# hl 32 bytes later, and the two weight slots apart by 64 bytes modulo 128

## The chip, the cores and the metric

The kernel runs on one core of one Trainium2 chip. The metric is the device time of one execution in microseconds, the median of several runs. The core has five engines with a queue each: TensorE (PE, with PEld for the loading of weights into the array), VectorE (DVE), ScalarE (ACT), GpSimd (POOL) and SyncE (SP, which here only issues DMAs). The working memory (SBUF) has 128 partitions; a tile takes the same bytes of each, and this case is about the byte at which a tile begins in its partition.

## The reference

One encoder layer (D_MODEL 1024, depth 1) is applied to two sequences of 1024 tokens, each with a conditioning vector. Cut to what matters:

```
mod = silu(c) @ w_ada + b_ada ; shift, scale, gate = split(mod, 3)
h = rmsnorm(x, norm_g) * (1 + scale) + shift
a_b, a_c, a_x, a_z, q, k, v, b_z, lr_f, lr_b, m_a, m_b = split(h @ w_in)
y_a = (a_b * conv3(a_c * a_x) * silu(a_z)) @ w_a_out
o = gla(q, k, v, g_f) + flip(gla(flip(q), flip(k), flip(v), flip(g_b), strict))
y_b = (rmsnorm(o) * gla_norm_g * silu(b_z)) @ w_b_out
x = x + gate * ((sigmoid(m_a) * y_a + sigmoid(m_b) * y_b) @ w_out)
y = rmsnorm(x, final_norm_g)
```

`gla` is a gated linear attention with 4 heads (keys of 128, values of 256 per head), g_f and g_b its log decays from a low-rank product. All is float32.

## The kernel before

Every large product is made in three matmuls on float32r operands: a float32 value is split into a high part (rounded by ScalarE, L114) and a low part (the rest, subtracted by VectorE or GpSimd, L115). `product` (L127) issues for each 128 rows of the contraction `hi.hi` (L131), `hi.lo` (L132) and `lo.hi` (L133); the first operand is the weights that are loaded into the array, the second the moving one. `mm3` (L135) runs it over the 8 blocks k of the model dimension.

- **hh and hl** (L97, L98) are the high and low parts of the modulated h, features in the partitions, 8 x 1024 float32 each, 32 KB a partition. They live through the whole kernel: for sequence 0, then 1, and at the end they hold w_out. `h_act` gives the slices.
- **w** (L118, `load_w`): 128 output columns of a weight matrix at a time, loaded into `raw` (three slots, by SP's queue), split into w's high and low half, 4 KB each. The tag "w" has two slots (NW), used in turn. `halves` (L141) makes one such tile's product with 2 x 512 tokens: for each 512 tokens 24 matmuls of 128 weight columns by 512 moving columns into one PSUM bank, so 48 matmuls use one slot. `wlr` (L427) is a narrow tile of the same tag.
- **big and small** (L66, L69): ten slots of 8 KB and eight of 4 KB, for all else: wv (values' weights, which are the moving operand there, with hh and hl as weights and 256 columns), b (the operands of the output products in `merge`, L691), mg (weights in `final`, L740), V, kt, As, SB, SF, Q (attention), wf and wa (start).
- **ones** and ident are constants, in a pool of their own ahead of hh. `over_features` (L166) sums over the partitions by a matmul with ones as weights.

The order of the work: `start` (modulation, h of sequence 0, and the first products as h arrives), then for each sequence `mixers` (four heads; each head's projections, then its attention, into which steps of the convolution's projections, `dense`, are woven) and `merge` (output products and gates, while h of the next user is filled into hh and hl), then `final`. A tile framework allocates the pools one tag after the other in the order in which they first appear, and makes every wait from what the tiles read and write. Weights are prefetched by giving `load_w` a higher priority.

Of the kernel before, what the change touches and what calls it, by code (L numbers as in the profile page):

```python
# [11 lines left out]
F32 = mybir.dt.float32  # L12
F32R = mybir.dt.float32r
# [4 lines left out]
P = 128  # L18
D = 1024
KT = D // P  # L20
L = 1024
# [16 lines left out]
NBIG, NSMALL, NW, NRAW = 10, 8, 2, 3  # L38
# [13 lines left out]
def encoder_kernel(ctx, tc, x_p, x_s, x_t, weights, w_lr, w_gate, w_out, vectors, b_gate, final_norm_g, masks, y_p, y_s):  # L52
# [6 lines left out]
    sb = ctx.enter_context(tc.tile_pool(name="sb", bufs=1))  # L59
# [35 lines left out]
    mk = const.tile([P, len(MASKED), P], U8, name="mk")  # L95
    sel = sb.tile([4, 2], F32, name="sel")
    hh = sb.tile([P, KT, L], F32R, name="hh")  # L97
    hl = sb.tile([P, KT, L], F32R, name="hl")  # L98

    ta_d = [dram.tile([KT, P, L], F32, name=f"ta_d{s}") for s in range(2)]  # L100
# [5 lines left out]
    def staged(src, shape=(P, L), queue=lambda load: None):  # L106

        raw = sb.tile(list(shape), F32, name="raw", tag="raw", bufs=NRAW)
        queue(nc.sync.dma_start(out=raw, in_=src))
        return raw  # L110

    def split(hi, lo, raw, engine):

        high = nc.scalar.copy(out=hi, in_=raw)  # L114
        engine.tensor_sub(out=lo, in0=raw, in1=hi.bitcast(F32))  # L115
        return high

    def load_w(i, shape=(KT, P), w=None, **kw):  # L118

        with tc.high_priority(offset=30):  # L120
            if w is None:
                w = sb.tile([P, 2, *shape], F32R, name="w", tag="w", bufs=NW)
            raw = staged(weights[i].rearrange("p (k c) -> p k c", c=shape[1]), (P, *shape), **kw)
            split(w[:, 0], w[:, 1], raw, nc.vector)
        return w[:, 0], w[:, 1]
# [15 lines left out]
    def halves(i, use, act=h_act, w=None):  # L141

        hi, lo = w or load_w(i)
        for t in range(2):
            sl = slice(t * HALF, (t + 1) * HALF)
            ps = dense_ps()
            for ks in (range(KT // 2), range(KT // 2, KT)):
                mm3(ps, lambda k: (hi[:, k, :], lo[:, k, :]), lambda k: act(k, sl), ks=ks,
                    first=(ks[0] == 0), last=(ks[0] > 0))
                if ks[0]:  # L150
                    use(ps, sl)
                yield
# [69 lines left out]
    def start():  # L222
# [58 lines left out]
        def weights_of(i):  # L281
            first.append(load_w((W_AC, W_AX, W_AZ)[i], w=big("wf", F32R, (P, 2, KT, P)) if i == 2 else None, queue=queue))
# [229 lines left out]
    def values(state, h):  # L512
        V = state["V", h] = big("Vh", F32R, (P, TB, DV)), big("Vl", F32R, (P, TB, DV))
        w = [load_w(W_V + 2 * h + kg, (4, DV), big("wv", F32R, (P, 2, 4, DV))) for kg in range(2)]
        yield
        for g in range(TB // 2):
            ps = psd.tile([P, 2, DV], F32, name="ps")
            for b in range(2):
                ts = slice((2 * g + b) * P, (2 * g + b + 1) * P)
                mm3(ps[:, b, :], lambda k: h_act(k, ts), lambda k: (w[k // 4][0][:, k % 4, :], w[k // 4][1][:, k % 4, :]))  # L520
                if b:
                    gs = slice(2 * g, 2 * g + 2)
                    split(V[0][:, gs, :], V[1][:, gs, :], ps, nc.vector)
                yield
# [321 lines left out]
```

## Time and profile before

| | |
|---|---|
| median of 3 runs | 2451.97 us (2451.96 to 2452.18) |
| the profiled execution | 2453.73 us |
| its span, first to last instruction | 2451.6 us |
| PE, matmuls | 2413.9 us busy, 12233 |
| PEld, weight loads | 2037.7 us busy, 12233 |
| DVE / ACT / POOL | 1210.3 / 851.9 / 229.0 us busy |
| mean granted TensorE clock | 0.994 |

Matmuls are pipelined: a row of the timeline gives 0.39 us to a matmul of 512 columns though the next one starts 0.23 us after it, so their busy times overlap, and a pace is read from starts. A 512-column matmul needs 213.3 ns for its columns at 2.4 GHz. In the page's chain of work each step is followed back to what released it; the shares say which engine's work made up the time. The times in a row of grouped instructions are the sum, the mean of one in ns, and the idle time of the engine just before them with what ended it.

### The profile page before, as it was taken

The page shows a single profiled execution, that of the slowest core. Times are in us where ns is not written, and L with a number is a line of the kernel's source. Part 1 is how long each engine was busy: PE and PEld are TensorE (multiplying, and loading weights), DVE is VectorE, ACT ScalarE, POOL GpSimd, SP SyncE. Part 2 cuts the span into 40 slices and gives each one's busy share as a digit, 9 for nine tenths or more (in the row PEclk, how much of TensorE's full clock was granted, in tenths as well). Part 3 has the DMA queues.
Part 4 walks back from the last instruction along what each step waited for, and adds up shares of the span by engine and source line. Part 5 has one row for each costly group of instructions (what it writes and reads, how often), then busy time and mean ns, then how long its engine had stood idle before and what let it go on. Part 6 is the DMA issues. An engine that isn't in the chain of part 4 may idle for free.

```text
span 2451.6 us, 28938 instructions
## 1 busy us (share of the span) xinstructions
PE 2413.9 (98%) x12233; PEld 2037.7 (83%) x12233; DVE 1210.3 (49%) x1412; ACT 851.9 (35%) x1276; POOL 229.0 (9%) x171
## 2 busy tenths in 40 slices
PE   7999999999999999999999999999999999999998
PEld 4788888888888888888888888888888888888887
DVE  6647567567367411324466466466466411323333
ACT  5443463443433311212523523524524311212221
POOL 3101001001001000011001001001001000012421
PEclk8999999999999999999999999999999999999999
DMA  6201311311211411423201201201201411324541
GB/s 248 76 26 35 112 69 52 129 69 44 69 35 44 138 52 44 129 80 135 78 31 48 78 26 52 78 26 52 78 26 52 138 44 51 129 103 137 189 137 61
DMA packets 68322, 196.24 MB, mean 80 GB/s; under 512 B 5824, under 2 KB 22816, under 8 KB 68192
## 3 DMA queue, kind: packets, MB, share of 16 engines
q1 hardware_dynamic: 60704, 167.51, 20.2%
q10 hardware_dynamic: 7488, 26.87, 2.9%
q8 instruction: 96, 1.57, 0.3%
q14 instruction: 34, 0.28, 0.0%
HBM read 159.24 MB, written 35.13 MB: 79 GB/s over the span
## 4 chain that ended last, share of the span: by engine, by line
PE 94%; DVE 3%; issue 1%; ACT 1%; DMA 1%; POOL 0%; SPq 0%; POOLq 0%; DVEq 0%; ACTq 0%
PE ps L131 28%; PE ps L133 28%; PE ps L132 28%; PE pl L553 3%; PE pm L131 2%; PE pm L132 1%; PE pm L133 1%; PE pl L170 1%; PE ps L437 1%; PE pm L684 1%; PE pm L620 0%; DVE As L115 0%; DVE w L115 0%; PE pm L218 0%; DMA araw<-in_weights_dram 0%
## 5 line engine op out<-in xcount | busy, mean ns | idle before, releaser
L131 PE MATMUL ps<-hh,w 128*128 128x512 f32 x2032 | 801.2, 394 | 4.4 <-ACT hh L189 4.4
L133 PE MATMUL ps<-hh,w 128*128 128x512 f32 x2032 | 794.2, 391 | 0.1
L132 PE MATMUL ps<-hl,w 128*128 128x512 f32 x2032 | 794.0, 391 | 0.0
L133 PEld LDWEIGHTS ps<-hh,w 128*128 128x128 f32 x2032 | 382.5, 188 | 80.9 <-DVE w L115 0.5
L131 PEld LDWEIGHTS ps<-hh,w 128*128 128x128 f32 x2032 | 383.0, 188 | 79.6 <-ACT hh L189 4.6
L132 PEld LDWEIGHTS ps<-hl,w 128*128 128x128 f32 x2032 | 383.2, 189 | 74.7
L115 DVE TENSOR_TENSOR w<-raw,w 128x1024 fp32r<-128x1024 f32 x159 | 210.8, 1326 | 271.2 <-ACT w L114 271.2
L114 ACT CAST w<-raw 128x1024 fp32r<-128x1024 f32 x159 | 166.4, 1047 | 374.0 <-PE ps L133 359.0
L131 PE MATMUL ps<-b,w 128*128 128x512 f32 x512 | 199.2, 389 | 0.0
L132 PE MATMUL ps<-b,w 128*128 128x512 f32 x512 | 199.2, 389 | 0.0
L133 PE MATMUL ps<-b,w 128*128 128x512 f32 x512 | 199.2, 389 | 0.0
L133 PE MATMUL ps<-wv,hl 128*128 128x256 f32 x512 | 144.9, 283 | 0.0
L132 PE MATMUL ps<-wv,hh 128*128 128x256 f32 x512 | 144.9, 283 | 0.0
L131 PE MATMUL ps<-wv,hh 128*128 128x256 f32 x512 | 144.9, 283 | 0.0
L457 POOL TENSOR_TENSOR u<-u,sg 128x512 f32<-128x512 f32 x32 | 45.8, 1432 | 1047.5 <-DVE sg L456 784.3
L702 ACT ACTIVATE sg<-ps 128x512 f32<-128x512 f32 x64 | 38.3, 598 | 244.5 <-PE ps L133 244.4
L131 PEld LDWEIGHTS ps<-b,w 128*128 128x128 f32 x512 | 96.1, 188 | 20.0
L132 PEld LDWEIGHTS ps<-b,w 128*128 128x128 f32 x512 | 96.1, 188 | 20.0
L133 PEld LDWEIGHTS ps<-b,w 128*128 128x128 f32 x512 | 96.1, 188 | 19.9
L726 POOL TENSOR_TENSOR sg<-m,sg 128x512 f32<-128x512 f32 x32 | 45.0, 1405 | 657.0 <-DVE sg L725 532.2
L132 PE MATMUL ps<-hl,mg 128*128 128x512 f32 (+1 forms) x264 | 101.0, 383 | 0.0
L133 PE MATMUL ps<-hh,mg 128*128 128x512 f32 (+1 forms) x264 | 101.0, 383 | 0.0
(217 smaller groups left out, 3253.6 us busy)
## 6 DMA issues: line engine op xcount, KB each, us to landing
raw<-in_weights_dram SPq DMA_DIRECT2D x184, 512.0 KB, 3.3
araw<-in_weights_dram SPq DMA_DIRECT2D x16, 512.0 KB, 4.5
ta_d<-u ACTq DMA_DIRECT2D x16, 512.0 KB, 2.7
ob_d<-sz ACTq DMA_DIRECT2D x16, 512.0 KB, 3.8
raw<-ta_d SPq DMA_DIRECT2D x16, 512.0 KB, 4.1
raw<-ob_d SPq DMA_DIRECT2D x16, 512.0 KB, 3.5
mg_d<-sg ACTq DMA_DIRECT2D x16, 512.0 KB, 3.1
raw<-mg_d SPq DMA_DIRECT2D x16, 512.0 KB, 4.2
```

Source lines behind the costliest of these rows:

```text
L114: high = nc.scalar.copy(out=hi, in_=raw)
L115: engine.tensor_sub(out=lo, in0=raw, in1=hi.bitcast(F32))
L131: nc.tensor.matmul(out, ahi, bhi, start=(first and i == 0), stop=False)
L132: nc.tensor.matmul(out, ahi, blo, start=False, stop=False)
L133: nc.tensor.matmul(out, alo, bhi, start=False, stop=(last and i == n - 1))
L170: nc.tensor.matmul(out(t), ones if x.dtype == F32R else ones.bitcast(F32), x[:, t * HALF:(t + 1) * HALF], start=(first and i == 0), stop=( ...
L437: nc.tensor.matmul(ps[:4 * RANK], w[:, k, :], h, start=(k + i == 0), stop=(k * i == KT - 1))
L457: nc.gpsimd.tensor_mul(out=u[:, sl], in0=u[:, sl], in1=sg[:, sl])
L553: nc.tensor.matmul(pl[:, j * P:(j + 1) * P], km[:, c * P:(c + 1) * P], qm(c), start=True, stop=True)
L684: nc.tensor.transpose(out=tp[:, b * P:(b + 1) * P], in_=ot[:, b, j * P:(j + 1) * P], identity=ident)
L702: run(halves(W_MA + i, lambda ps, sl: nc.scalar.activation(out=sg[:, sl], in_=ps, func=AF.Sigmoid)))
L726: nc.gpsimd.tensor_add(out=g[:, sl], in0=m1[f][:, sl], in1=g[:, sl])
```

## The change

A tile of 8 float32, 32 bytes, is allocated between hh and hl and never used. And a slot of w is made 16 float32, 64 bytes, longer than its content: the tile is allocated flat, and the view of the old shape is taken from its first 8192 bytes. Every other line is the same.

```
     hh = sb.tile([P, KT, L], F32R, name="hh")
+    sb.tile([P, 8], F32, name="gap")
     hl = sb.tile([P, KT, L], F32R, name="hl")
...
             if w is None:
-                w = sb.tile([P, 2, *shape], F32R, name="w", tag="w", bufs=NW)
+
+                slot = sb.tile([P, 2 * L + 16], F32R, name="w", tag="w", bufs=NW)
+                w = slot[:, :2 * L].rearrange("p (a k c) -> p a k c", a=2, k=shape[0])
             raw = staged(weights[i].rearrange("p (k c) -> p k c", c=shape[1]), (P, *shape), **kw)
```

The built programs have the same instructions in the same order on every engine, with the same shapes; the tiles' numbers of slots are the same. What differs is the byte of the partition at which tiles begin (in brackets: modulo 128):

| tile | before | after |
|---|---|---|
| ident, ones | 16512, 17664 (both 0) | the same |
| hh | 19040 (96) | 19040 (96) |
| hl | 51808 (96) | 51840 (0) |
| every slot of `small` and `big` | from 84576 (all 96) | 32 bytes later (all 0) |
| w, slot 0 | 199264 (96) | 199296 (0) |
| w, slot 1 | 207456 (96) | 207552 (64) |
| raw, three slots | from 215648 (all 96) | from 215808 (all 0) |

Slices of these tiles (a block k, a half of the tokens, the high or the low half) lie apart by multiples of 128 bytes, so they begin at the same place modulo 128 as their tile.

## Rows read from the trace of the kernel before

**Rows 1.** The page: busy times of the engines, and its chain by engine and line

```profile
PE 2413.9 (98%) x12233; PEld 2037.7 (83%) x12233; DVE 1210.3 (49%) x1412; ACT 851.9 (35%) x1276; POOL 229.0 (9%) x171
...
PE 94%; DVE 3%; issue 1%; ACT 1%; DMA 1%; POOL 0%; SPq 0%; POOLq 0%; DVEq 0%; ACTq 0%
PE ps L131 28%; PE ps L133 28%; PE ps L132 28%; PE pl L553 3%; PE pm L131 2%; PE pm L132 1%; PE pm L133 1%; PE pl L170 1%; PE ps L437 1%; PE pm L684 1%; PE pm L620 0%; DVE As L115 0%; DVE w L115 0%; PE pm L218 0%; DMA araw<-in_weights_dram 0%
```

**Rows 2.** Windows: stretch, its length, busy us by engine (instructions), clock, DMA share, GB/s

```profile
828.00:1172.00 344.00, 344.00 (x1519) 284.87 (x1518) 104.80 (x96) 74.48 (x87) 19.97 (x14) 1.00 0.29 98
1172.00:1900.00 728.00, 728.00 (x3981) 628.54 (x3981) 414.01 (x504) 293.65 (x456) 54.21 (x35) 1.00 0.15 52
```

**Rows 3.** Timeline of PE, first merge: start, us, line, out<-in, shapes; 195 starts apart

```profile
999.79 0.39 PE L131 MATMUL ps<-hh,w 128*128 128x512 f32 x1
...
1043.99 0.39 PE L131 MATMUL ps<-b,w 128*128 128x512 f32 x1
```

**Rows 4.** Timeline of PE, values of sequence 1: 100 starts apart

```profile
1204.96 0.28 PE L131 MATMUL ps<-wv,hh 128*128 128x256 f32 x1
...
1216.96 0.28 PE L132 MATMUL ps<-wv,hh 128*128 128x256 f32 x1
```

**Rows 5.** Groups of PE by line and form: operands, shapes, count | busy, mean ns | idle

```profile
L131 PE MATMUL ps<-hh,w 128*128 128x512 f32 x2032 | 801.2, 394 | 4.4 <-ACT hh L189 4.4
...
L132 PE MATMUL ps<-hl,w 128*128 128x512 f32 x2032 | 794.0, 391 | 0.0
L131 PE MATMUL ps<-b,w 128*128 128x512 f32 x512 | 199.2, 389 | 0.0
...
L131 PE MATMUL ps<-wv,hh 128*128 128x256 f32 x512 | 144.9, 283 | 0.0
...
L132 PE MATMUL ps<-hl,mg 128*128 128x512 f32 x248 | 96.5, 389 | 0.0
...
L131 PE MATMUL pm<-Vh,kt 128*128 128x256 f32 x112 | 33.8, 302 | 0.0
...
L131 PE MATMUL pm<-Vh,As 128*128 128x256 f32 x64 | 18.0, 282 | 0.4 <-DVE st L642 0.4
...
L131 PE MATMUL pm<-SBh,Qh 128*128 128x256 f32 x56 | 15.8, 283 | 0.0
```

**Rows 6.** Timeline of PE where ones are weights, first head of sequence 0

```profile
180.34 0.40 PE L133 MATMUL ps<-hh,w 128*128 128x512 f32 x1
180.58 0.63 PE L170 MATMUL pl<-Xh,ones 128*128 128x512 f32 x2
181.04 0.62 PE L170 MATMUL pl<-Xl,ones 128*128 128x512 f32 x2
181.51 0.40 PE L131 MATMUL ps<-hh,w 128*128 128x512 f32 x1
...
182.66 0.40 PE L133 MATMUL ps<-hh,w 128*128 128x512 f32 x1
```

**Rows 7.** Timeline of PE, the low-rank product with wlr: 11 starts apart

```profile
105.34 0.40 PE L437 MATMUL ps<-hh,wlr 128*64 128x512 f32 x1
...
107.87 0.39 PE L437 MATMUL ps<-hl,wlr 128*64 128x512 f32 x1
```

**Rows 8.** Timeline of PE, modulation: 16 matmuls with weights of 4 columns, and the next

```profile
74.45 2.03 PE L218 MATMUL pm<-wa,scs 128*4 128x256 f32 x16
76.32 0.39 PE L131 MATMUL ps<-hh,w 128*128 128x512 f32 x1
```

**Rows 9.** Groups by line and form: the splits of w

```profile
L115 DVE TENSOR_TENSOR w<-raw,w 128x1024 fp32r<-128x1024 f32 x159 | 210.8, 1326 | 271.2 <-ACT w L114 271.2
...
L114 ACT CAST w<-raw 128x1024 fp32r<-128x1024 f32 x159 | 166.4, 1047 | 374.0 <-PE ps L133 359.0 <-DMA raw<-in_weights_dram 7.6 <-issue 7.3
```

**Rows 10.** The page's DMA issues: out<-in, queue, count, KB each, median us to landing

```profile
raw<-in_weights_dram SPq DMA_DIRECT2D x184, 512.0 KB, 3.3
```

## The prediction

> **What bounds the kernel now.** I read the page's busy shares and its chain first. TensorE's matmuls are busy 98% of the span, and 94% of the chain that ended last is PE, nearly all of it the three lines of `product`, L131 to L133 [rows 1]. The windows by stage say the same: from 828 to 1172 us, with a granted clock of 1.00 (the 2.4 GHz level), PE is busy for all of the 344 us [rows 2]. So no other engine, no DMA and no wait has anything to give there. What is left is the time from one matmul's start to the next one's. The busy column can't show it, since matmuls overlap and it says 0.39 us for each; the starts do. In the timeline 195 matmuls of 512 columns start between 999.79 and 1043.99 us: 44.20 / 195 = 226.7 ns each [rows 3]. 512 columns at 2.4 GHz take 213.3 ns, so each matmul has 13.3 ns on top. For 256 columns, 100 matmuls start within 12.00 us: 120.0 ns against 106.7, again 13.3 on top [rows 4]. The excess is the same for both sizes: some 12,000 matmuls at 13 ns hold about 160 us of the span. The change can only matter through it.
>
> **The change part by part.** No instruction is added, removed or moved; every engine has the same sequence. What changes is where tiles begin in a partition. Before, hh, hl, both slots of w and every tile that comes out of `big` and `small` begin at byte 96 modulo 128. After, hh is still at 96; hl, w's slot 0 and all `big` and `small` tiles are at 0; w's slot 1 is at 64. The gap stands ahead of hl, but everything allocated behind hl is moved with it, so b, wv, mg and the V and S tiles move as well.
>
> (a) *The splits and the loads.* ScalarE's cast and VectorE's subtract into w (159 each, 1047 and 1326 ns [rows 9]) and the loads into raw (3.3 us from issue to landing [rows 10]) get other addresses. Their cover is PE's own stream: ScalarE sits idle 374.0 us ahead of those casts, 359.0 of it waiting for PE to free a slot, and PE's idle time ahead of its commonest line is 4.4 us in the whole span [rows 5, 9]. I take nothing. If each split became longer by a tenth, 159 x 0.24 = 38 us of other engines' time would still lie under a PE that runs without a gap.
>
> (b) *Moving operands that now begin at a multiple of 64.* The excess says something about how they are read. 13.3 ns is 32 columns, or 128 bytes of fp32. A stream of 2048 bytes that begins at 96 modulo 128 touches 17 pieces of 128 bytes instead of 16, and one of 1024 bytes touches 9 instead of 8: 17 x 32 columns are 544, or 226.7 ns, and 9 x 32 are 288, or 120.0 ns. Both measured values come out. It isn't proof, since a fixed cost of 32 columns fits as well. What speaks for a part of it: with weights of 4 columns, which take next to nothing to load, 16 matmuls of 256 columns still need 1.87 us, 116.9 ns each, 10 above the columns' own time [rows 8]; so most of the excess isn't the loading of the next weights. The bounds for an operand that moves from 96 to 0 are therefore 0 (fixed cost) and 13.3 ns (one piece of 128 bytes less); I take the half, 6.7 ns, which is one piece of 64 bytes less, because the row of 10 lies between and a part of it may be fixed. Matmuls with such a moving operand: hl with w 2032 and with mg 248; b 3 x 512; wv 3 x 512; Vh and Vl with kt 3 x 112 and with As 3 x 64; SB and SF 6 x 56 [rows 5], where one row stands for each three equal groups. That makes 6216, and 6216 x 6.7 = 41 us gained (0 to 83).
>
> (c) *The weights against the moving operand.* Before, both begin at the same place modulo 128. The only weights in the trace that don't are `ones`, at 0 while X and hh are at 96. In the run of 226.7 ns the matmul under which `ones` is loaded first takes 180.58 - 180.34 = 0.24 us, and five from there take 181.51 - 180.34 = 1.17 us, 234 ns each; the five after it, with w at 96 again, take 1.15 us, 230 each [rows 6]. The matmuls with `wlr` (64 columns, all at 96) never settle: 11 in 2.53 us, 230 ns each [rows 7]. So 226.7 is a pace that matmuls settle into, and out of it they cost 3 to 7 ns more. After the change w's slot 0 stands to hh as `ones` stands to X; slot 1 stands to hh as nothing in the trace does; hl to slot 0 and b to slot 0 stand as before. Matmuls that stream hh: 2 x 2032 with w and 2 x 248 with mg (L131 and L133), 4560 in all. I price them at +3.3 ns, the pace of the longest row out of step, since the 234 also holds the first step of a disturbance: 4560 x 3.3 = 15 us lost. The bounds are -13 ns (a better pace, none of the rows) and +7.3 ns: -60 to +33 us.
>
> [...]
>
> **The sum.** Profiled span 2451.6 us, about 2.1 us less than that execution's 2453.73 us; the median of the runs is 2451.97, 1.8 us below that execution. From the median: 2452 - 41 + 15 = 2426; I say 2425.
>
> **The rivals.**
>
> *It ends slower.* The mechanism is (c) without (b): the excess is a fixed cost, nothing is gained by the new begins, and the products of hh and hl lose the settled pace, because in each three matmuls the operand's begin now changes (96, 0, 96) and w's slot 0 is off by 32 bytes. The place is all of L131 to L133 with w and mg: 3 x 2032 + 3 x 248 = 6840 matmuls, at +3.3 to +7.3 ns: +23 to +50 us, in the middle 2452 + 34 = 2486. It decides once the loss on the 4560 matmuls of hh is above 41 us, 9 ns each, or once (b) gives less than 15 us, 2.4 ns each. For it: the `ones` rows are the only look at such a begin, and they are slower. Against it: they are a handful of matmuls just after a disturbance.
>
> *Nothing changes.* The pace doesn't hang on the begin at all; the row of `ones` shows something else (another region of the memory, another PSUM pool), and 226.7 stands: 2452. For it: 226.7 holds through all k and both halves, over 30 KB of hh and with weights at either end of the memory. Against it: the step to 0.24 us comes just where the begin differs. [...]
>
> *It doesn't do what it says.* "hl later, the slots apart" is only a part of it: all that lies behind hl moves. Were the gain only for hl and hh's own products, (b) would shrink to 2280 matmuls, 15 us, and with (c) the sum would be 0; this is a way to the second rival's time and is counted there.
>
> **How the numbers follow.** Faster, by (b) larger than (c): 0.48, around 2425; with the half of (b) or all of it and (c) from +33 to 0, this case reaches from 2447 down to 2370, but the far end needs the whole 13.3 ns and a pace for hh that no row shows. Slower: 0.38, from 2457 (a loss that (b) partly makes up for) to 2502. Within 0.2% (4.9 us, about what a measurement can tell here): 0.14; it holds the second rival and sums that cancel. The range is 2405 to 2488: it leaves out the far end of the gain (under 0.1) and the upper third of the slower case (about 0.1). The likeliest case's own range is 2405 to 2447.
>
> **What would show it.** In the trace after, I would read starts, not busy time. (b): in the merge stage, where 24 matmuls of b with w follow each other, the pace goes from 226.7 to about 220; with wv from 120.0 to about 113. If these stand at 226.7 and 120.0, (b) is wrong. (c): within a three of L131, L132, L133 the steps differ, the ones that stream hh at about 230. If all are 226.7, begins don't matter and the second rival holds. If slot 0 and slot 1 of w have different paces, the begin of the weights against the operand is what counts. The prediction fails if hh, hl and w go at 230 or more while b stays at 226.7. DVE, ACT and DMA rows should stand as before; if w's splits were longer and PE waited for them, (a) was wrong.

## The result, and the profile after

| | before | after |
|---|---|---|
| median | 2451.97 us (4 runs, 2449.96 to 2452.18) | 2486.27 us (4 runs, 2485.32 to 2486.87) |
| profiled execution, its span | 2453.73, 2451.6 us | 2486.63, 2484.5 us |
| PE busy | 2413.9 us | 2447.4 us |

The changed kernel is slower: ratio 1.0141, 95% interval 1.0124 to 1.0159, or 34.3 us. The forecast was 2425, faster; the slower rival had 2486.

The page and the windows of after answer to [rows 1, 2]. The windows' columns are the stretch, its length, busy time by engine (PE, PEld, DVE, ACT, POOL) with counts, the granted clock, the DMA share and GB/s.

```profile
PE 2447.4 (99%) x12233; PEld 2032.5 (82%) x12233; DVE 1209.1 (49%) x1412; ACT 852.6 (34%) x1276; POOL 230.0 (9%) x171
...
PE 95%; DVE 2%; issue 1%; ACT 1%; DMA 1%; POOL 0%; SPq 0%; POOLq 0%; DVEq 0%; ACTq 0%
```

```profile
828.00:1172.00 344.00, 344.00 (x1503) 281.08 (x1503) 99.23 (x93) 70.84 (x83) 17.65 (x13) 1.00 0.29 98
1172.00:1900.00 728.00, 728.00 (x3921) 618.60 (x3920) 412.79 (x494) 291.55 (x442) 53.97 (x33) 1.00 0.15 52
```

The bound is the same: PE never waits in these stretches, at the same granted clock of 1.00. It starts 1503 matmuls in the 344 us where it started 1519. The totals of DVE, ACT and POOL moved by 1.2 us at most. So each matmul got longer, and the question is which.

The groups by form answer to [rows 5] and, for the splits, [rows 9]:

```profile
L134 PE MATMUL ps<-hh,w 128*128 128x512 f32 x2032 | 811.9, 400 | 4.3 <-ACT hh L192 4.3
L136 PE MATMUL ps<-hh,w 128*128 128x512 f32 x2032 | 805.3, 396 | 0.1
L135 PE MATMUL ps<-hl,w 128*128 128x512 f32 x2032 | 800.7, 394 | 0.0
L116 DVE TENSOR_TENSOR w<-raw,w 128x1024 fp32r<-128x1024 f32 x159 | 211.2, 1329 | 279.9 <-ACT w L115 279.8
L134 PE MATMUL ps<-b,w 128*128 128x512 f32 x512 | 201.1, 393 | 0.0
...
L134 PE MATMUL ps<-hh,mg 128*128 128x512 f32 x248 | 98.4, 397 | 0.0
...
L135 PE MATMUL ps<-hl,mg 128*128 128x512 f32 x248 | 97.5, 393 | 0.0
```

The splits stand (1329 against 1326 ns). Everything of 512 columns has a longer mean, b too, but a mean over 2032 mixes slots. The starts tell them apart. In the first merge the matmuls of b have w's slot 0 and those of hh and hl slot 1; in the second merge it is the other way round (but for a tile or two at the ends). The timeline of PE (start, duration in us, line, operands), always two starts of 36 matmuls apart within one tile of weights: first b with slot 0, then hh and hl with slot 1; then, second merge, b with slot 1 and hh and hl with slot 0.

```profile
987.41 0.39 PE L134 MATMUL ps<-b,w 128*128 128x512 f32 x1
...
995.57 0.39 PE L134 MATMUL ps<-b,w 128*128 128x512 f32 x1
...
998.33 0.39 PE L134 MATMUL ps<-hh,w 128*128 128x512 f32 x1
...
1006.68 0.39 PE L134 MATMUL ps<-hh,w 128*128 128x512 f32 x1
...
2053.30 0.40 PE L134 MATMUL ps<-b,w 128*128 128x512 f32 x1
...
2061.70 0.40 PE L134 MATMUL ps<-b,w 128*128 128x512 f32 x1
2064.50 0.40 PE L134 MATMUL ps<-hh,w 128*128 128x512 f32 x1
...
2072.90 0.40 PE L134 MATMUL ps<-hh,w 128*128 128x512 f32 x1
```

That is 8.16, 8.35, 8.40 and 8.40 us for 36: b with slot 0 at 226.7 ns as in [rows 3], hh and hl with slot 1 at 231.9, b with slot 1 at 233.3, hh and hl with slot 0 at 233.3. (All 32 tiles of a merge go like these, but for one in the second: hh and hl with slot 0 right behind a tile with slot 1, at 231.1.) Only b with slot 0, whose begins are both at 0, kept the settled pace. The values of 256 columns went the other way, 100 starts in 11.77 us, 117.7 ns each against 120.0 [rows 4]:

```profile
1214.67 0.28 PE L134 MATMUL ps<-wv,hh 128*128 128x256 f32 x1
...
1226.44 0.28 PE L135 MATMUL ps<-wv,hh 128*128 128x256 f32 x1
```

For the whole span I took the step from each matmul's start to the next one's, all 12,233 in both traces, grouped by stream and weights, and subtracted the sums:

| stream, weights | matmuls | mean step before | after | change |
|---|---|---|---|---|
| hh, w | 4064 | 232.9 ns | 238.2 ns | +21.5 us |
| hl, w | 2032 | 229.6 | 232.7 | +6.2 |
| b, w | 1536 | 226.7 | 230.4 | +5.7 |
| hh, mg | 496 | 226.5 | 234.5 | +3.9 |
| hl, mg | 248 | 227.0 | 231.0 | +1.0 |
| wv, hh and hl | 1536 | 119.9 | 117.7 | -3.5 |

These make +34.8 us; all the rest is -1.9, and the spans differ by 32.9. The means of hh with w hold the steps in which PE waits for other work, so they lie above the settled pace in both kernels. What makes the 13.3 ns that the prediction sets beside the columns in these 226.7 stays open; the runs below are about what comes on top of 226.7.

### The profile page after: what moved, and what is told of

Read it like the earlier page. It is cut to its first block, busy times and chain, and to the rows that moved or that the text cites. A ratio compares the mean times of both kernels' runs of the same rounds, so it can differ in the third digit from the quotient of the medians.

```text
span 2484.5 us, 28938 instructions
## 1 busy us (share of the span) xinstructions
PE 2447.4 (99%) x12233; PEld 2032.5 (82%) x12233; DVE 1209.1 (49%) x1412; ACT 852.6 (34%) x1276; POOL 230.0 (9%) x171
## 4 chain that ended last, share of the span: by engine, by line
PE 95%; DVE 2%; issue 1%; ACT 1%; DMA 1%; POOL 0%; SPq 0%; POOLq 0%; DVEq 0%; ACTq 0%
PE ps L134 28%; PE ps L136 28%; PE ps L135 28%; PE pl L556 3%; PE pm L134 2%; PE pm L135 1%; PE pm L136 1%; PE pl L173 1%; PE ps L440 1%; PE pm L687 1%; PE pm L623 0%; DVE As L116 0%; DMA araw<-in_weights_dram 0%; PE pm L221 0%; DVE w L116 0%
## 5 line engine op out<-in xcount | busy, mean ns | idle before, releaser
L134 PE MATMUL ps<-hh,w 128*128 128x512 f32 x2032 | 811.9, 400 | 4.3 <-ACT hh L192 4.3
L136 PE MATMUL ps<-hh,w 128*128 128x512 f32 x2032 | 805.3, 396 | 0.1
L135 PE MATMUL ps<-hl,w 128*128 128x512 f32 x2032 | 800.7, 394 | 0.0
L136 PEld LDWEIGHTS ps<-hh,w 128*128 128x128 f32 x2032 | 382.3, 188 | 91.9 <-DVE w L116 0.5
L134 PEld LDWEIGHTS ps<-hh,w 128*128 128x128 f32 x2032 | 382.9, 188 | 86.2 <-ACT hh L192 4.5
L135 PEld LDWEIGHTS ps<-hl,w 128*128 128x128 f32 x2032 | 382.6, 188 | 84.6
L116 DVE TENSOR_TENSOR w<-raw,w 128x1024 fp32r<-128x1024 f32 x159 | 211.2, 1329 | 279.9 <-ACT w L115 279.8
L134 PE MATMUL ps<-b,w 128*128 128x512 f32 x512 | 201.1, 393 | 0.0
L135 PE MATMUL ps<-b,w 128*128 128x512 f32 x512 | 201.1, 393 | 0.0
L136 PE MATMUL ps<-b,w 128*128 128x512 f32 x512 | 200.9, 392 | 0.0
L134 PE MATMUL ps<-wv,hh 128*128 128x256 f32 x512 | 143.5, 280 | 0.0
L135 PE MATMUL ps<-wv,hh 128*128 128x256 f32 x512 | 143.5, 280 | 0.0
L136 PE MATMUL ps<-wv,hl 128*128 128x256 f32 x512 | 143.4, 280 | 0.0
L134 PEld LDWEIGHTS ps<-b,w 128*128 128x128 f32 x512 | 96.2, 188 | 21.9
L136 PEld LDWEIGHTS ps<-b,w 128*128 128x128 f32 x512 | 96.2, 188 | 21.8
L135 PEld LDWEIGHTS ps<-b,w 128*128 128x128 f32 x512 | 96.2, 188 | 21.8
L134 PE MATMUL ps<-hh,mg 128*128 128x512 f32 (+1 forms) x264 | 102.9, 390 | 0.0
L136 PE MATMUL ps<-hh,mg 128*128 128x512 f32 (+1 forms) x264 | 102.9, 390 | 0.0
```

What stands on the lines that cost most here:

```text
L134: nc.tensor.matmul(out, ahi, bhi, start=(first and i == 0), stop=False)
L135: nc.tensor.matmul(out, ahi, blo, start=False, stop=False)
L136: nc.tensor.matmul(out, alo, bhi, start=False, stop=(last and i == n - 1))
```

## Experiments

Each kernel below is the kernel before with the edit shown; where a removed line isn't one of the kernel before, the edit is to the kernel just above, or to the one that the text names. Places are given as the begin of the weights behind that of their stream, in bytes; the stream is the moving operand. A tile below is 48 matmuls that use one slot of w. The expectations name three theories. By R the pace of a matmul follows from that difference modulo 128, with some differences dear and some perhaps cheap. By S it follows from the step between the begins of two moving operands that follow each other. By E a stretch settles at 226.7 ns only where all begins are equal, and any departure slows it. R and E took a period of 128 bytes for granted at first.

A time in brackets is that of the kernel before on the same chip. But for the last of the kernels and the one with both distances at 256 bytes, each time is one run; the runs of the kernel before lie between 2449.38 and 2453.91 us, so a time alone tells nothing below some 4 us, and the paces have to carry the argument. The granted clock is 1.00 from 100 to 2400 us in the traces of before and after, and its mean over the span is 0.993 to 0.997 in every run, so differences in pace of 3% aren't the clock's.

### One part at a time: hl's gap, the slots, and everything later

The gap alone, without wider slots (all behind hl moves with it, as in the change):

```diff
     hh = sb.tile([P, KT, L], F32R, name="hh")
+    sb.tile([P, 8], F32, name="gap")
     hl = sb.tile([P, KT, L], F32R, name="hl")
```

> The gap ahead of hl alone: hh at 96, hl, b, wv and both slots of w at 0 (all modulo 128). Theory R (what counts is the begin of the weights less that of the operand that streams meanwhile): hh with w is at +32 throughout, hl and b with w at 0; from slot 0 of the changed kernel, three matmuls of hh, hl, hh take 16.5 ns more than before, 2032 x 16.5 = +33 us, mg +5, wv -4, b nothing: about 2486 us, and b with w at 226.7 ns in both slots. Theory S (what counts is the step between the begins of two operands that follow each other): hh to hl to hh is still 32 apart, so the same 2486 us. If the slots alone were to blame: 2452 us.

Measured 2483.99 us, beside 2450.44 for the kernel before on that chip. b goes at 226.7 with both slots, hh and hl at 233.3 with both. R and S both said so; the next run tells them apart.

The wider slots alone:

```diff
-                w = sb.tile([P, 2, *shape], F32R, name="w", tag="w", bufs=NW)
+                slot = sb.tile([P, 2 * L + 16], F32R, name="w", tag="w", bufs=NW)
+                w = slot[:, 0:2 * L + 0].rearrange("p (a k c) -> p a k c", a=2, k=shape[0])
```

> The longer slot alone: everything at 96 but slot 1 of w, at 32. Theory R: slot 0 as before; slot 1 stands 64 off hh, hl and b, as b with slot 1 in the changed kernel, which took 233.2 ns against 226.7: 3048 matmuls of hh and hl at +5 to +6.5 and 768 of b at +6.5, +20 to +25 us: about 2474 us. Theory S: the moving operands are untouched: 2452 us.

Measured 2472.12 (2450.44). Its timeline, two starts of 36 matmuls apart for hh and hl with slot 1, then for b with slot 0:

```profile
995.49 0.39 PE L132 MATMUL ps<-hh,w 128*128 128x512 f32 x1
...
1003.89 0.39 PE L132 MATMUL ps<-hh,w 128*128 128x512 f32 x1
...
1006.65 0.39 PE L132 MATMUL ps<-b,w 128*128 128x512 f32 x1
...
1014.81 0.39 PE L132 MATMUL ps<-b,w 128*128 128x512 f32 x1
```

8.40 us is 233.3 ns, 8.16 is 226.7. No moving operand has moved, so S can't be the cause here. Either part alone costs: +33.5 and +21.7 us. Together they cost 34.3, not 55, because the products of hh and hl with slot 1 are out of step in each and can't be so twice. By the sums of steps, the change has 5.7 us on b where the gap alone has 1.2, but 27.8 on hh and hl with w where the gap alone has 32.3, since with slot 1 they go at 231.9 ns and not at 233.3.

Everything later, with the gap ahead of hh, so that all operands begin at 0 modulo 128 and stand to each other as before:

```diff
+    sb.tile([P, 8], F32, name="gap")
     hh = sb.tile([P, KT, L], F32R, name="hh")
```

> The gap ahead of hh: hh, hl, w, raw and all of big and small 32 bytes later, at 0 modulo 128; only ones, ident and what else lies ahead of hh stay. Theory E: nothing is out of step with anything, 226.7 ns for all 512-column products, 120.0 for wv: 2450 us. The prediction's step (b), that a stream which begins at a multiple of 64 saves a piece: 220 ns or less: about 2410 us.

Measured 2450.27 (2450.06). The timeline: hh and hl, 36 starts apart, and the values, 100 apart:

```profile
987.99 0.39 PE L132 MATMUL ps<-hh,w 128*128 128x512 f32 x1
...
996.15 0.39 PE L132 MATMUL ps<-hh,w 128*128 128x512 f32 x1
...
1203.85 0.28 PE L132 MATMUL ps<-wv,hh 128*128 128x256 f32 x1
...
1215.85 0.28 PE L133 MATMUL ps<-wv,hh 128*128 128x256 f32 x1
```

8.16 us for 36 and 12.00 for 100: 226.7 and 120.0 to the digit, with every begin at 0 where it was at 96. So 32 bytes more on every operand cost and give nothing; a price comes only with where one begins against another.

### The size of the difference

Weights 64 bytes later, all of them (and 128 spare bytes to a slot):

```diff
-                w = sb.tile([P, 2, *shape], F32R, name="w", tag="w", bufs=NW)
+                slot = sb.tile([P, 2 * L + 32], F32R, name="w", tag="w", bufs=NW)
+                w = slot[:, 16:2 * L + 16].rearrange("p (a k c) -> p a k c", a=2, k=shape[0])
```

> Both slots of w begin 64 bytes later than before, at 32 modulo 128, all else at 96. Theory R: twice the loss of the slots alone, in both slots: +40 to +50 us, about 2497 us, b with w at 233 in both slots. Theory S: 2452 us.

Measured 2482.5 (2450.44), between S's time and R's. And 96 bytes later, which is 32 back modulo 128:

```diff
-                w = slot[:, 16:2 * L + 16].rearrange("p (a k c) -> p a k c", a=2, k=shape[0])
+                w = slot[:, 24:2 * L + 24].rearrange("p (a k c) -> p a k c", a=2, k=shape[0])
```

> Both slots of w begin 96 bytes later, which is 32 ahead of the others modulo 128 (64 against 96). In the changed kernel wv streams at 0 while hh, the weights there, is at 96: the same relation, and its 256-column matmuls went from 120.0 to 117.5 ns. Theory R: if a gain of 2.5 ns per matmul holds for 512 columns, 6096 + 1536 matmuls x 2.5 = -19 us, about 2433 us, the pace of b at 224; if the relation has another best place for 512 columns, another time than 2452, but the same for hh, hl and b. Theory S: 2452 us, 226.7.

Measured 2499.5. R's gain isn't there; hh, hl and b are all at 233 ns or above in the merges. A map of eight places in steps of 16 bytes, taken in turn by the tiles of weights:

```diff
-                w = sb.tile([P, 2, *shape], F32R, name="w", tag="w", bufs=NW)
+                slot = sb.tile([P, 2 * L + 32], F32R, name="w", tag="w", bufs=NW)
+                o = 4 * (i % 8)
+                w = slot[:, o:2 * L + o].rearrange("p (a k c) -> p a k c", a=2, k=shape[0])
```

> Each tile of w begins 0, 16, 32 ... 112 bytes later than its slot, by its index modulo 8; hh, hl, b and the slots are at 96 as before, so one run shows the pace of b with w at eight relations in steps of 16 bytes. Theory R: 226.7 ns at 0, 233 at +64, 234 at +96 as in the runs before, +32 near 233; the four new places lie at 230 to 236 if 0 is the only place that settles, and at 224 or less if there is a better one. The total has no forecast but the mean of its places: about 2485 us if 0 alone is good.

Measured 2481.16 (2449.38). And one with places a few bytes apart:

```diff
-                o = 4 * (i % 8)
+                o = (0, 1, 2, 3, 5, 6, 30, 31)[i % 8]
```

> The same with 0, 4, 8, 12, 20, 24 bytes later and 8 and 4 bytes earlier (modulo 128). [...]

Measured 2477.09 (2449.38). No place of either map is below 226.7 ns. But a place did not have one pace: in the second map 8 of the 20 tiles of b at 0 and 4 or 8 bytes around it went at 226.7 ns and 12 at 230.6 to 233.3. Two kernels that move a part of the change with another were as odd. The low parts of w moved 32 bytes along with hl:

```diff
+    sb.tile([P, 8], F32, name="gap")
     hl = sb.tile([P, KT, L], F32R, name="hl")
+    sb.tile([P, 24], F32, name="gap2")
...
-                w = sb.tile([P, 2, *shape], F32R, name="w", tag="w", bufs=NW)
+                slot = sb.tile([P, 2 * L + 32], F32R, name="w", tag="w", bufs=NW)
+                w = slot[:, :2 * (L + 8)].rearrange("p (a c) -> p a c", a=2)[:, :, :L]
+                w = w.rearrange("p a (k c) -> p a k c", k=shape[0])
```

> hl 32 bytes later as in the change, all behind hl put back to 96 by a second gap, and the low half of each w tile 32 bytes later as well. While hl streams, the low half is loaded; while hh streams, the high half. Theory R (the stream against the load beneath it): all three matmuls of a product of hh and hl are at relation 0 again, 226.7 ns, though hh, hl, hh begin 32 apart; only b's low part (+32 against w's low half) and hl with mg (-32) are off, one matmul of three, +3 ns each of some 2300: about 2459 us. If the step between successive moving operands counts (theory S), or the weights that the matmul itself uses, the dense products stay at 231 to 234 ns: 2475 to 2490 us.

Measured 2483.64 (2449.38), against R. Then hl alone 32 bytes later, all behind it by 128, w as before:

```diff
+    sb.tile([P, 8], F32, name="gap")
     hl = sb.tile([P, KT, L], F32R, name="hl")
+    sb.tile([P, 24], F32, name="gap2")
```

> hl 32 bytes later and nothing else: a second gap of 96 bytes behind hl puts all that follows back to 96. While hl streams, w is loaded at -32; while hh streams, at 0. If only the stream against the load beneath it counted (theory R), one matmul of three would be off, at 234 ns, the others at 226.7: 2032 x 7.3 + 248 x 7.3 = +17 us, 2467 us. Theory E (the settled pace needs hh, hl and both halves of w at the same place modulo 128, and any one tile off unsettles all three matmuls): the dense products at 231 to 234, some +5.5 ns x 6840 = +38 us, about 2488 us; b with w at 226.7 in both.

Measured 2464.95 (2450.06): near R's figure, but not in R's way, since in the merges two of each three went at 229 to 231 ns, and not hl alone above 226.7. Last, a grid of 64 pairs of places for the high and the low parts in steps of 16 bytes (each pair once in the merges), with the low part 128 bytes behind the high part's end and slots 256 bytes wider:

```diff
+    places = [(4 * a, 4 * b) for a in range(8) for b in range(8)]
+    turn = [0]
...
-                w = sb.tile([P, 2, *shape], F32R, name="w", tag="w", bufs=NW)
+                slot = sb.tile([P, 2 * L + 64], F32R, name="w", tag="w", bufs=NW)
+                a, b = 0, 0
+                if W_MA <= i < W_ADA:
+                    a, b = places[turn[0] % 64]
+                    turn[0] += 1
+                hi, lo = (slot[:, o:o + L].rearrange("p (k c) -> p k c", k=shape[0]) for o in (a, L + 32 + b))
...
```

> In merge, the 64 weight tiles of both sequences get the 64 pairs of places of w's high and low half in steps of 16 bytes, hh, hl and b at 96 as before; outside merge w stays as before. Theory E: 226.7 ns only where both halves are within some 8 bytes of the operands' place, 229 to 236 in all other pairs, mean 232: the merges' 3072 matmuls +5.3 ns, about 2467 us. If another pair gives a settled pace below 226.7 (a sum of three matmuls below 680 ns), the rival is that equal places are just one of several good ones, and such a pair is the better layout.

Measured 2480.96 (2450.06). Of the 64 tiles of the merges one settled at 226.7 (high part equal, low part 16 bytes off by my count, 144 in truth), the rest went at 228.9 to 235.6, among them the one that I had counted as equal, at 231. Nor did w stay as before outside the merges: its low part lay 128 bytes further there too, which the expected time had left out.

In all of these the slots, or the low parts, or everything behind hl had been put 128 bytes further, which I had taken for no change. They have that in common.

### The period

Slots 512 bytes wider, so that both stand alike, and the weights in steps of 64 bytes over 512:

```diff
-                w = sb.tile([P, 2, *shape], F32R, name="w", tag="w", bufs=NW)
+                slot = sb.tile([P, 2 * L + 128], F32R, name="w", tag="w", bufs=NW)
+                o = 16 * ((i // 2) % 8)
+                w = slot[:, o:2 * L + o].rearrange("p (a k c) -> p a k c", a=2, k=shape[0])
```

> Here the slots of w get 512 spare bytes each, so that both slots stand to hh, hl and b as before modulo 512, and successive pairs of weights begin 0, 64, 128, ... 448 bytes into their slot; nothing else moves. So each of eight relations of weights to stream occurs in both slots, with hh and hl and with b. If a settled pace of 226.7 ns needs equal begins modulo 128, the relations 0, 128, 256 and 384 settle and the time is about 2473 us (half of 7632 products at +5.5 ns). If modulo 256, only 0 and 256 settle: about 2483. If modulo 512, only 0 settles: about 2489. In each case the tiles of the other relations go at 229 to 236 ns. If the placement in equal steps of 64 did not matter, all would be at 226.7 and the time 2452.

Measured 2473.52 (2451.02). The timeline, two starts of 36 matmuls apart in five tiles: weights at 256 (b), 320 (b), 448 (hh), 0 (hh), 128 (hh).

```profile
874.16 0.39 PE L133 MATMUL ps<-b,w 128*128 128x512 f32 x1
...
882.32 0.39 PE L133 MATMUL ps<-b,w 128*128 128x512 f32 x1
...
918.66 0.39 PE L133 MATMUL ps<-b,w 128*128 128x512 f32 x1
...
927.06 0.39 PE L133 MATMUL ps<-b,w 128*128 128x512 f32 x1
...
952.12 0.39 PE L133 MATMUL ps<-hh,w 128*128 128x512 f32 x1
...
960.37 0.39 PE L133 MATMUL ps<-hh,w 128*128 128x512 f32 x1
...
996.22 0.39 PE L133 MATMUL ps<-hh,w 128*128 128x512 f32 x1
...
1004.38 0.39 PE L133 MATMUL ps<-hh,w 128*128 128x512 f32 x1
...
1106.76 0.41 PE L133 MATMUL ps<-hh,w 128*128 128x512 f32 x1
...
1115.13 0.40 PE L133 MATMUL ps<-hh,w 128*128 128x512 f32 x1
```

226.7, 233.3, 229.2 (228.9 before rounding), 226.7, 232.5 ns. All tiles of the merges, worked out the same way:

| weights behind the stream, bytes | pace, ns |
|---|---|
| 0, 256 | 226.7 in all 16 tiles |
| 64, 320 | 233.3 to 233.4 |
| 128, 384 | 232.3 to 232.6 |
| 192, 448 | 228.9 |

It is the same in both slots, with b and with hh and hl. In this run the period is 256 bytes. The whole time came out where a period of 128 had been expected, in part because I had priced every unequal place at 5.5 ns, and 192 costs only 2.2: 256 was to cost 4.1 ns a matmul in the mean, the trace has 3.2. Read by its time alone this run would have been misread.

Modulo 256 all operands of the products begin at 96 in the kernel before. After the change hh is at 96, hl, b, mg, wv and slot 0 are at 128, slot 1 at 192: 32 and 96 against hh, 0 and 64 against hl and b. With a period of 256 the earlier runs fall into place, though not wholly. In the two maps, which have four tiles at each of 32 places, all four have one pace within 0.4 ns at 26 of the places, whichever the slot and the stream. But at 16 and at 144 bytes one tile of four went at 226.7, right behind a tile that had settled, and the other three, behind tiles that had not, at 233.3. And in the kernel with all weights 64 bytes later slot 1 stands at 192: there 16 tiles went at 228.9 and 16 at 233.3, the two in turn, as in these two of hh and hl from the first merge (8.24 and 8.40 us for 36):

```profile
865.27 0.39 PE L132 MATMUL ps<-hh,w 128*128 128x512 f32 x1
...
873.51 0.39 PE L132 MATMUL ps<-hh,w 128*128 128x512 f32 x1
...
887.50 0.40 PE L132 MATMUL ps<-hh,w 128*128 128x512 f32 x1
...
895.90 0.40 PE L132 MATMUL ps<-hh,w 128*128 128x512 f32 x1
```

So an unequal place doesn't fix the pace by itself. The settled tiles in front speak for something that is carried on from the matmuls before; no run shows it.

With that, hl alone again, all behind it by 512 bytes now:

```diff
-    sb.tile([P, 24], F32, name="gap2")
+    sb.tile([P, 120], F32, name="gap2")
```

> hl begins 32 bytes later, and all behind it 512 bytes later, so that w, b, mg and wv stand to hh and to each other exactly as before modulo 512: hl alone is out of step. Theory E (a place in the three at which the begins differ disturbs all three matmuls): the threes of L131 to L133 sum to 700 ns in place of 680, as in the changed kernel, 2280 threes x 20 ns = 46 us: about 2488 to 2498 us. Theory R (only the matmul whose stream and whose next weights differ is longer): 2280 matmuls of hl at +5 to +7 ns, 11 to 16 us: 2463 to 2468 us, with sums of three of 685 to 687 ns. b, wv and wlr stay at 226.7, 120.0 and 230 by both. If the 128 bytes by which w stood off hh were what cost time when hl was moved alone with 128 bytes behind it, this run is faster than that one's 2465.

Measured 2474.7 (2451.02), between the two theories. The groups by form:

```profile
L134 PE MATMUL ps<-hl,mg 128*128 128x512 f32 x248 | 97.9, 395 | 0.0
L133 PE MATMUL ps<-hh,mg 128*128 128x512 f32 x248 | 97.7, 394 | 0.0
L135 PE MATMUL ps<-hh,mg 128*128 128x512 f32 x248 | 97.3, 392 | 0.0
```

Against 389 for each before [rows 5], hl has the most, but its neighbours, whose own begins are equal, lose 5 and 3 ns too. In the merges a three settles at 695 ns in all tiles but the first two of each, which with the same places have 700, as the change has with slot 0. So neither R (one matmul) nor E (the full loss) is right as it stood: the matmul out of step is longer, and those beside it lose too, by less.

Next comes the changed kernel itself with both of its distances made 256 bytes:

```diff
-    sb.tile([P, 8], F32, name="gap")
+    sb.tile([P, 64], F32, name="gap")
...
-                slot = sb.tile([P, 2 * L + 16], F32R, name="w", tag="w", bufs=NW)
+                slot = sb.tile([P, 2 * L + 64], F32R, name="w", tag="w", bufs=NW)
```

> The changed kernel with both distances made 256 bytes: hl and all behind it begin 256 bytes later, and the slots of w lie 256 bytes apart modulo 512. If only the begins modulo 256 count, all products settle at 226.7 ns and those of 256 columns at 120.0, and the time is that of the kernel before, within 0.1% (2450 to 2454). If the relation counts modulo 512, or if the gap or the width of the slots costs something by itself, hh and hl go at 229 ns or more: 2465 us or more.

Measured 2450.71 us (10 runs) beside 2450.52 (13 runs): ratio 1.0000, interval 0.9990 to 1.0009. hh and hl, 36 starts apart:

```profile
1006.10 0.39 PE L134 MATMUL ps<-hh,w 128*128 128x512 f32 x1
...
1014.26 0.39 PE L134 MATMUL ps<-hh,w 128*128 128x512 f32 x1
```

226.7 again. The gap, the wider slots and the move of everything behind them cost nothing; the 32 and the 64 bytes do.

### Which weights, and whether another place holds

The low parts of w alone 64 bytes later (the slots 256 wider, so that they stand alike):

```diff
-                w = sb.tile([P, 2, *shape], F32R, name="w", tag="w", bufs=NW)
+                slot = sb.tile([P, 2 * L + 64], F32R, name="w", tag="w", bufs=NW)
+                hi, lo = (slot[:, o:o + L].rearrange("p (k c) -> p k c", k=shape[0]) for o in (0, L + 16))
...
```

> The low parts of w begin 64 bytes later against hh, hl, b and the high parts; the slots lie equal modulo 256, nothing else moves (wv, mg, V and S keep their places). The three of L133, L134, L135 uses the weights high, high, low. If the weights that a matmul uses matter, the third matmul (L135) is the long one, +5 to +7 ns. If the weights that are loaded while it streams matter, the second (L134: hl, or b's low part) is the long one, and L133 and L135 stay at 226.7. Either way, one matmul of three: 2544 x 5 to 7 ns = 13 to 18 us, 2464 to 2469 us. If, as with hl alone, the other two of the three lose as well (a three at 695 ns), 2544 x 15 = 38 us: up to 2489.

Measured 2476.15 (median of before 2453.12). In its groups by form L134 and L135 use the high part and L136 the low one (the expectation's L133 to L135 are these three):

```profile
L136 PE MATMUL ps<-b,w 128*128 128x512 f32 x512 | 203.5, 397 | 0.0
L135 PE MATMUL ps<-b,w 128*128 128x512 f32 x512 | 200.7, 392 | 0.0
L134 PE MATMUL ps<-b,w 128*128 128x512 f32 x512 | 199.2, 389 | 0.0
```

Before, each had 389 [rows 5]. The long one is the one that uses the shifted weights; their load is recorded while L135 streams (in the trace of before, L133's load starts at 1000.02 us and takes 0.19, while L132 starts at 1000.02 and L133 at 1000.25), and L135 has only 3 ns more. By the starts in ns the three goes 228, 229, 236, sum 693. So if the recorded starts are those of the streams, it is the weights a matmul uses that count against its stream. That is argued from the records and not shown by a second run, and what the chip does there isn't shown by any: the loads of w are recorded at 188 or 189 ns in the mean in before, after and this kernel.

In the maps some tiles at other places than 0 had gone at 226.7, at +132 bytes all four of the merges (and at +120 and +252, which no further run tried). hh and hl put 124 bytes later against all else (modulo 256) puts every product of theirs at +132:

```diff
-    hh = sb.tile([P, KT, L], F32R, name="hh")
-    hl = sb.tile([P, KT, L], F32R, name="hl")
+    sb.tile([P, 24], F32, name="gap")
+    hh = sb.tile([P, KT * L + 8], F32R, name="hh")[:, 7:KT * L + 7].rearrange("p (k c) -> p k c", k=KT)
+    sb.tile([P, 56], F32, name="gap2")
+    hl = sb.tile([P, KT * L + 8], F32R, name="hl")[:, 7:KT * L + 7].rearrange("p (k c) -> p k c", k=KT)
+    sb.tile([P, 32], F32, name="gap3")
```

> hh and hl begin 124 bytes later, all else 512 bytes later: w and mg begin 132 bytes behind hh and hl modulo 256, b and w stay equal, wv as weights' partner is off by 124. In the map in steps of 4 bytes all four tiles at +132 settled at 226.7. If that relation is a second settled place, hh and hl go at 226.7, b too, and the 1536 matmuls of wv with hh and hl go at about 118 in place of 120: 2452 - 3 = 2449 us, a little better than both kernels. If only equal begins settle for good and the tiles of the map were led into 226.7 by those before them, the products of hh and hl go at 230 to 233 ns: 6840 x 4 to 6.7 = 27 to 46 us, 2479 to 2498.

Measured 2468.28 (4 runs) beside 2453.12 (7 runs), ratio 1.0058, interval 1.0042 to 1.0075. hh and hl settle at 230.0 ns (36 starts apart):

```profile
996.26 0.39 PE L134 MATMUL ps<-hh,w 128*128 128x512 f32 x1
...
1004.54 0.39 PE L134 MATMUL ps<-hh,w 128*128 128x512 f32 x1
```

8.28 us for 36. So +132 isn't a settled place here: the pace is the low end of the second expectation, and the time, 2468, lies below its range. The place +132 can hold 226.7 and does not always; what decides it is open. Equal begins settled at 226.7 ns in every tile of the merges, in all twelve kernels that have them; +120 and +252 did too, but in one kernel, with four tiles each. I found no layout that beats the kernel before.

## Why the prediction was wrong

**What bounds the kernel.** Right: PE without gaps, and the change acts through the time from one start to the next alone. The 13.3 ns beside the columns were the right place to look, though they are an estimate: no trace has the columns' time by itself. The paces of 512 and 256 columns differ by 226.7 - 120.0 = 106.7 ns at a granted clock of 1.00, which is 2.4 columns per ns; if what comes on top is the same for both, 213.3 of the 226.7 are the columns' and 13.3 are left.

**(a) Splits and loads at nothing.** Right: 1329 against 1326 ns, and DVE's total is 1.2 us lower.

**(b) 41 us gained by moving operands at a multiple of 64.** This is the step that failed. "17 pieces of 128 bytes instead of 16" fitted both paces of before, and I had written that a fixed cost of 32 columns fits as well; then I took half. With every operand at 0 (everything later) the paces are 226.7 and 120.0: the excess doesn't follow an operand's own begin. b with slot 0 in the changed kernel says the same. So the 41 us measured 0. The row that I used as a support [rows 8] doesn't choose between a fixed cost and pieces; and its loads of 4 columns, which I called next to nothing, are recorded at 96 ns each in the mean, against 188 for 128 columns. The gain that came, 2.3 ns on the 1536 matmuls of wv, isn't (b): with wv at 0 and in step it is absent (120.0), so it comes from being out of step.

**(c) 15 us lost by hh against the weights.** The mechanism was right, the term mis-sized. The change in the steps of hh is 21.5 + 3.9 us over 4560 matmuls, 5.6 ns each instead of 3.3. Missing were hl, 6.2 + 1.0 us (equal to slot 0 but not to slot 1, and between two matmuls of hh that are out of step), and b with slot 1, 5.7 us. I had counted hl and b only by slot 0. These terms alone are 38 us; less the 3.5 of wv they make the loss. The row behind the price was luck in part: modulo 256 `ones` stand 160 bytes behind X, and slot 0 stands 32 behind hh, another place that happens to be dear too (233.3 ns in the second merge, against 234 in [rows 6]). And [rows 7] are no row of a new place, since `wlr` and its streams begin alike; why they go at 230 is open.

**The rivals.** "It ends slower" is what happened, by its mechanism, (c) without (b), with its place and a fitting price: 4.8 ns on its 6840 matmuls, within 3.3 to 7.3. Of its two reasons the runs show the weights that stand off their stream; the change of begin between streams is not needed, since the wider slots cost 21.7 us without one, and no run shows it by itself. That its 2486 is the measured time is luck: the middle of +23 to +50 is 36 and not 34, and it left out b's 5.7 and wv's -3.5. "Nothing changes" is refuted: b with slot 1 went from 226.7 to 233.3 ns where nothing but begins changed. Whether the loads of weights take the 5.6 ns from hh's matmuls no run shows; with the low parts shifted the matmul over their load lost 3 ns and the one that uses them 8.

**The reading that was within reach.** [Rows 6] had the only operands at a new place against each other, and they were slower; no row had any that were faster. The gain in (b) had no row in which a begin alone differed. A term with a row should have gone ahead of one with only a fitting sum, and 0.48 against 0.38 should have been the other way round.

## What to carry to other kernels

Where PE runs without a gap, read its pace from starts, and check what all operands' begins are against each other before a layout is changed: here weights of 128 columns and streams that begin alike modulo 256 bytes keep 512 columns at 226.7 ns, and 32 or 64 bytes between them cost up to 3% of each matmul (233.3 ns). In a kernel like this one, pad tiles by multiples of 256 bytes, not of 32 or 64. When two explanations fit a constant, find or make the run that moves one of them alone before a gain is booked on it, and read paces beside the time, since in one run here the right time came from the wrong theory.

## What the runs showed of the hardware

- The pace of a 512-column matmul of these products depends on where its weights begin against its stream: 226.7 ns at 0 and 256, 233.3 at 64 and 320, 232.3 to 232.6 at 128 and 384, 228.9 at 192 and 448 in one run, a period of 256 bytes. With both distances of the change made 256 the whole loss is gone (2450.71 us).
- It depends on more than that place: at 192 another kernel had 228.9 and 233.3 in turn.
- A common move of all operands by 32 bytes, from 96 to 0 modulo 128, changes nothing: 2450.27 us beside 2450.06.
- For 256 columns, out of step is faster: 117.7 against 120.0 ns for wv with hh and hl. In this layout wv lies in the tiles that b uses later, and b has to stand like w; no run tried to have its 3.5 us alone.
- With one matmul of three out of step the other two are longer too: 228, 229, 236 ns with the low parts of w shifted.
- At +132 bytes all four tiles of one kernel held 226.7 ns, and in another all tiles of hh and hl in the merges go at 230.0. Why is open.
